# First stage of a two-layer hybrid decoder: weight and modulation loads issued a quarter at a time

## The chip, the cores and the metric

The kernel runs on 1 core of one Trainium2 chip. The metric is the device time of one execution in microseconds (us); lower is better.

## The reference

Two layers, each with a token mixer and a gated MLP. Every sub-layer is wrapped in RMSNorms and modulated by shift, scale and gate, which come from a conditioning vector. All inputs are float32. What matters here is the beginning of layer 0:

```python
cond = jax.nn.silu(c)
mods = cond @ w_ada[l] + b_ada[l]
sh1, sc1, g1, sh2, sc2, g2 = [m[:, None, :] for m in jnp.split(mods, 6, axis=-1)]
h = rms_norm(x, norm_pre_mix[l]) * (1.0 + sc1) + sh1
proj = h @ w_in
```

`x` is 256 x 2048, `w_ada[l]` is 2048 x 12288, `w_in` is 2048 x 4564. The columns of `proj` go to four head groups: latent attention, S5 (a diagonal complex state space model), sparse attention and gated DeltaNet. The S5 group also needs tables that depend on parameters alone.

## The kernel before

The order of instructions on each engine is made by a scheduler from the order in which the program writes them, their dependencies and priorities; `order` below means its result. Each engine and each DMA queue then works in that order. All large loads are issued on SP's queue, as tiles of 128 x 1024 floats (512 KB).

**Modulation.** No column of `h` can be made before shift and scale are known, so the first stage works in four quarters of the model dimension, 512 columns each. `ada_quarter(q)` (L490) loads the 16 tiles of `w_ada` for quarter `q` (8 MB) and multiplies each on TensorE with the condition vector into a bank (`mx`, products 32x512); after the last tile ScalarE copies the bank (`hf<-mx`, L513), four small products with `ident2` turn it into columns, and `ada_out` (L521) adds biases into `mod`. It is a generator: it issues a tile's load and writes the tile's products right behind it, and yields after every second tile. The tiles lie in free pieces of the arena and in the pools `rawa`, `rawm` and `acc`, two buffers each.

**Norm.** `row_scale` (L606) loads `x` transposed (`xT`, four tiles), squares it on ScalarE (two buffers), sums it with products with `ones` on TensorE, takes the inverse root on VectorE and scales the four quarters of `xT` (`scale`, L621). `norm_quarter(q)` (L628) applies shift and scale to a quarter (`hf`) and splits it in a high and a low part (`ht`), by a cast on ScalarE (L423) and a subtraction on VectorE (L424).

**First products.** `first_gemms(0)` (L1475) multiplies five column blocks of `w_in` (the list `FIRST`), each by one weight tile per quarter: `gemms_b` (L730) calls `wtile`, that is `wload` (L402, a load into one of four `raw` buffers) and `wsplit` (L437, a cast into one of three `wh` buffers and a subtraction into one of three `wl`), and then 24 products 128x256 into `mm` (the fifth block into `mx`). With `tiles=True` it yields after each weight tile.

**The loop.** `run` (L1675) puts these together. For quarters 1 to 3 it interleaves them by hand: after each of the five weight tiles it steps the modulation generator of the next quarter once or twice, and the generators of the S5 tables (`s5_tables`, L1241) and rotations (`s5_rotations`, L1364, all on VectorE at line L1367) twice. The five weight tiles of quarter 3 are left to `mixers` (L1481), which begins with what is left of the first products, and goes on with 852-column loads of `w_in` for other head groups. From there on the modulation tiles of the other blocks are summed on VectorE in the background (`ada`, L467).

Of the kernel before, what the change touches and what calls it, by code (L numbers as in the profile page):

```python
# [21 lines left out]
P = 128  # L22
# [38 lines left out]
FIRST = (O_U, O_U + 256, O_GQ, O_GK, O_GV)  # L61
# [21 lines left out]
class Blocks:  # L83
# [3 lines left out]
    def __init__(self):  # L87
        self.at, self.n = {}, 0
# [104 lines left out]
class Ker:  # L193
    def __init__(self, ctx, tc, I, out):
        self.tc, self.nc, self.I, self.out = tc, tc.nc, I, out
        pool = lambda name, bufs, **kw: ctx.enter_context(tc.tile_pool(name=name, bufs=bufs, **kw))
        self.const = pool("const", 1)
        self.ar = self.const.tile([P, NA], F32, name="arena")
        self.x = self.ar[:, A_X:A_X + 4096].rearrange("p (t d) -> p t d", t=2)

        ht = self.const.tile([P, 8, 1024], F32, name="ht")
        self.ht = [ht[:, i] for i in range(8)]
        self.raw = pool("raw", 4)
        self.whp = pool("wh", 3)
        self.wlp = pool("wl", 3)
        self.rawa = pool("rawa", 2)
        self.rawm = pool("rawm", 2)
        self.accp = pool("acc", 2)
        self.small = pool("small", 2)
        self.mmp = pool("mm", 4, space=PSUM)  # L210
        self.mxp = [pool("mx%d" % i, 2, space=PSUM) for i in range(2)]
        self.lane = None
        self.turn = 0
        self.turn_ins, self.turn_tiles = (), 0
        self.norm_ins, self.add_rest = (), None
        self.bg = iter(())
        self.side = iter(())
        self.boost = 0
        self.bg_rate = 0.0
        self.rates = (0.0,) * 4  # L220
        self.bg_credit = 0.0
# [268 lines left out]
    def ada_quarter(self, q):  # L490

        nc = self.nc
        bank = self.mx()
        pools = ((self.rawa, "rawa"), (self.rawm, "rawm"), (self.accp, "acc"))
        free = [A_OT + 1024] + (AT[7:9] if q else []) + (AT[:4] if q < 3 else [])
        for kc in range(KT):
            n = kc % (len(free) + 6)
            if n < len(free):  # L500
                w = self.reg(free[n], 1024)(1024)
            else:
                pool, nm = pools[(n - len(free)) % 3]
                w = pool.tile([P, 1024], F32, name=nm, tag=nm)
            nc.sync.dma_start(w, self.blk("w_ada", 0, kc, 1, (q * 512, 512), (D + q * 512, 512)))
            for i in range(2):
                o = 64 * (kc % 2) + 32 * i
                self.mm(bank[o:o + 32], self.condz[:, kc], w[:, i * 512:(i + 1) * 512], kc < 2, kc >= KT - 2)
            if kc % 2 and kc < KT - 1:
                yield  # L510
        with self.first():
            r = self.small.tile([P, 512], F32, name="hf", tag="hf")
            nc.scalar.copy(r, bank)  # L513
            cols = self.mx(8)
            for c in range(4):
                self.mm(cols[:, 2 * c:2 * c + 2], r[:, c * P:(c + 1) * P], self.ident2[:, 0:64:32], True, True)
            cols = cols.rearrange("p (c i) -> p i c", i=2)
            for i in range(2):
                self.ada_out(0, 2 * i + q // 2, cols[:, i], 4 * (q % 2))
# [210 lines left out]
    def gemms_b(self, l, cols, nm, kc, tiles=False):  # L730


        kn = 1024 // (nm * P)
        parts = [[b[:, m * 256:(m + 1) * 256] for m in range(nm)] for _, b in cols]
        for kk in range(0, KT, kc):
            for (c0, _), ps in zip(cols, parts):
                for k0 in range(kk, kk + kc, kn):
                    w = self.wtile(self.blk("w_in", l, k0, kn, (c0, nm * P)))
                    for ki in range(kn):
                        k = k0 + ki  # L740
                        for m in range(nm):
                            o = (ki * nm + m) * P
                            self.mm3(ps[m], [i[:, o:o + P] for i in w], self.hk(k), k == 0 and m == 0,
                                     k == KT - 1 and m == nm - 1)
                    if tiles:
                        yield
            if not tiles:
                yield
        return parts
# [725 lines left out]
    def first_gemms(self, l):  # L1475
        if l:
            return self.gemms_b(l, [(c, self.mmt()) for c in FIRST[:3]], 2, KT // 4)
        self.lane = 0
        return self.gemms_b(l, [(c, self.mmt() if i < 4 else self.mx()) for i, c in enumerate(FIRST)], 2, KT // 4, True)

    def mixers(self, l, first):  # L1481
# [193 lines left out]
    def run(self):  # L1675
# [13 lines left out]
        a = self.ada_quarter(0)  # L1689
        next(a)  # L1690
        self.finish(constants)
        self.lane = 0
        self.row_scale()
        self.lane = 1
        self.finish(a)
        done = self.norm_quarter(0)
        with self.after(done):
            for i in range(1, 4):
                self.scale(i)
        tables = self.s5_tables(0, nc.scalar, self.ar[:, AT[6]:AT[6] + 1024])  # L1700
        rotations = self.s5_rotations(0, (self.ar[:, AT[4]:AT[4] + 1024], self.ar[:, AT[5]:AT[5] + 1024]))
        g = self.first_gemms(0)
        for q in range(1, 4):
            self.lane = 1
            a = self.ada_quarter(q)
            if q == 3:
                self.lane = 0
                with self.after(done):
                    self.finish(tables)
                self.lane = 1  # L1710
            n = len(FIRST)
            for i in range(n):
                next(g)
                for _ in range(8 * (i + 1) // n - 8 * i // n):
                    next(a, None)
                self.lane = 0
                with self.after(done):
                    for _ in range(2):
                        next(tables if q < 3 else rotations, None)
                self.lane = 1  # L1720
            done = self.norm_quarter(q)
        self.lane = 0
        with self.after(done):
            self.finish(rotations)
# [5 lines left out]
        for l in range(DEPTH):  # L1730
            self.set_bg(bg[2 * l], False)
            if l:
                h, g = self.pre_norm(l, 0), self.first_gemms(l)
# [53 lines left out]
```

## Time and profile before

| | us |
|---|---|
| median of 3 runs | 2699.17 (2696.71 to 2700.51) |
| the profiled execution | 2692.16 |
| its span, first to last instruction | 2690.0 |
| TensorE busy | 2571.7 (96%) |
| VectorE busy | 1910.7 (71%) |
| ScalarE busy | 1259.9 (47%) |
| mean granted clock of TensorE | 0.978 |

The profile is of one execution. PE is TensorE, PEld its weight loads, DVE VectorE, ACT ScalarE, POOL GpSimd, SP the queue of loads (SPq). PEclk is the granted clock of TensorE in a stretch, 1.00 for 2.4 GHz and 0.50 for 1.2 GHz. A busy share of TensorE over the whole span says little about a stage: the first 200 us are looked at by stretches.

### The profile page before, as it was taken

The numbers are of one execution on the slowest core, as the hardware profiler recorded it, in microseconds if no ns is written. First come the engines' busy times: TensorE is split into PE (matmuls) and PEld (weight loads), VectorE is DVE, ScalarE is ACT, GpSimd is POOL, SyncE is SP. The second block draws the span as 40 slices with busy tenths as digits, with TensorE's granted clock in tenths as the row PEclk, the third lists the DMA queues.
The fourth block names the chain that finished last, engine by engine and source line by source line (L and its number), as shares of the span: only waits on it lengthen the run. The fifth ranks groups of instructions, "written<-read, shape, count | busy, mean of one in ns | idle before, by whom it ended". The sixth has DMA issues, their size and how long they took to land. (4 is left out here: it accounts for less than half of the span.)

```text
span 2690.0 us, 44478 instructions
## 1 busy us (share of the span) xinstructions
PE 2571.7 (96%) x17604; PEld 2285.0 (85%) x17604; DVE 1910.7 (71%) x3014; ACT 1259.9 (47%) x2002; POOL 10.1 (0%) x22
## 2 busy tenths in 40 slices
PE   7979998888999999999998999999899999999998
PEld 4568786767999999988887879888899999998886
DVE  5568867878787778776877888865776655555555
ACT  3344454555445444454545445465544444444443
POOL 0000000000000000000000000000000000000000
PEclk9989998889999999999998999999999999999999
DMA  8765756676888888876676567735587655555554
GB/s 343 313 212 198 256 197 210 220 266 216 291 297 277 289 289 298 291 242 234 229 269 216 176 218 248 254 114 180 186 283 270 209 185 183 182 184 186 185 189 147
DMA packets 171264, 620.89 MB, mean 231 GB/s; under 512 B 19440, under 2 KB 20272, under 8 KB 169520
## 3 DMA queue, kind: packets, MB, share of 16 engines
q1 hardware_dynamic: 170048, 617.00, 67.1%
q8 instruction: 138, 2.26, 0.3%
q10 hardware_dynamic: 1008, 1.06, 0.1%
q14 instruction: 70, 0.57, 0.1%
HBM read 613.75 MB, written 4.23 MB: 230 GB/s over the span
## 5 line engine op out<-in xcount | busy, mean ns | idle before, releaser
L228 PE MATMUL mm<-ht,wh 128*128 128x256 f32 x7168 | 1314.9, 284 | 6.7 <-ACT ht L423 5.8
L423 ACT CAST wh<-raw 128x1024 fp32r<-128x1024 f32 (+1 forms) x740 | 771.5, 1043 | 960.9 <-PE mm L228 785.0
L424 DVE TENSOR_TENSOR wl<-raw,wh 128x1024 fp32r<-128x1024 f32 (+1 forms) x740 | 896.6, 1214 | 404.5 <-ACT wh L423 401.0
L228 PEld LDWEIGHTS mm<-ht,wh 128*128 128x128 f32 x7168 | 1112.3, 189 | 22.8 <-issue 7.6
L228 PE MATMUL mm<-ht,wl 128*128 128x256 f32 x3584 | 1018.1, 284 | 2.4 <-DVE wl L424 2.4
L228 PEld LDWEIGHTS mm<-ht,wl 128*128 128x128 f32 x3584 | 675.3, 188 | 10.5 <-DVE wl L424 6.2
L228 PE MATMUL mm<-wh,ht 128*128 128x512 f32 (+1 forms) x1600 | 508.0, 396 | 8.0 <-ACT ht L423 4.2
L462 DVE SCALAR_TENSOR_TENSOR acc<-rawa,condc,acc 128x1024 f32<-128x1024 f32 x300 | 384.6, 1282 | 138.2 <-DMA rawa<-in_w_ada_dram 136.8
L228 PEld LDWEIGHTS mm<-wh,ht 128*128 128x128 f32 x1600 | 303.1, 191 | 72.3 <-ACT ht L423 4.5
L228 PE MATMUL mm<-wl,ht 128*128 128x512 f32 (+1 forms) x800 | 316.2, 395 | 0.0
L228 PE MATMUL mx<-arena 128*128 128x128 f32 (+9 forms) x1576 | 235.1, 320 | 18.9 <-DVE arena L373 10.0
L228 PEld LDWEIGHTS mx<-arena 128*128 128x128 f32 (+5 forms) x1576 | 164.8, 169 | 72.5 <-issue 20.4
L228 PE MATMUL mx<-wh,ht 128*128 128x512 f32 x704 | 222.3, 396 | 0.0
L228 PEld LDWEIGHTS mm<-wl,ht 128*128 128x128 f32 x800 | 152.6, 191 | 31.5 <-issue 0.2
L228 PEld LDWEIGHTS mx<-wh,ht 128*128 128x128 f32 x704 | 132.6, 188 | 32.3
L228 PE MATMUL mx<-wl,ht 128*128 128x512 f32 x352 | 139.5, 396 | 0.0
L424 DVE TENSOR_TENSOR ht<-arena,ht 128x1024 fp32r<-128x1024 f32 x52 | 63.6, 1223 | 40.4 <-ACT ht L423 40.1
L1615 DVE SCALAR_TENSOR_TENSOR arena<-mm,vec,arena 128x255 f32<-128x255 f32 (+1 forms) x176 | 78.5, 478 | 6.2 <-ACT arena L1613 5.3
L423 ACT CAST ht<-arena 128x1024 fp32r<-128x1024 f32 x52 | 54.2, 1049 | 56.1 <-PE mm L228 30.5
L228 PEld LDWEIGHTS mx<-wl,ht 128*128 128x128 f32 x352 | 66.3, 188 | 16.2
L232 PE MATMUL mx<-ident,arena 128*128 128x128 f32 (+1 forms) x328 | 59.4, 287 | 13.4 <-ACT arena L815 5.5
L232 PEld LDWEIGHTS mx<-ident,arena 128*128 128x128 f32 (+1 forms) x328 | 38.4, 144 | 29.9 <-ACT arena L815 9.8
(314 smaller groups left out, 1516.4 us busy)
## 6 DMA issues: line engine op xcount, KB each, us to landing
raw<-in_ffn_w_in_dram SPq DMA_DIRECT2D x352, 512.0 KB, 4.2
rawa<-in_w_ada_dram SPq DMA_DIRECT2D x330, 512.0 KB, 5.0
raw<-in_ffn_w_out_dram SPq DMA_DIRECT2D x176, 512.0 KB, 4.3
raw<-in_w_in_dram SPq DMA_DIRECT2D x116, 512.0 KB, 4.3
raw<-in_w_out_dram SPq DMA_DIRECT2D x64, 512.0 KB, 4.1
arena<-in_w_ada_dram SPq DMA_DIRECT2D x36, 512.0 KB, 7.8
raw<-in_w_in_dram SPq DMA_DIRECT2D x32, 426.0 KB, 3.9
rawm<-in_w_ada_dram SPq DMA_DIRECT2D x9, 512.0 KB, 9.3
```

Of the source, the lines that this page charges most:

```text
L228: self.nc.tensor.matmul(out, lhsT=lhsT, rhs=rhs, start=start, stop=stop)
L232: self.nc.tensor.transpose(out, in_, self.ident[:k, :k])
L423: self.nc.scalar.copy(hi.bitcast(F32R), src)
L424: self.last_lo = self.nc.vector.tensor_sub(lo.bitcast(F32R), src, hi)
L462: self.nc.vector.scalar_tensor_tensor(acc, w, self.condc[:, kc:kc + 1], acc, op0=ALU.mult, op1=ALU.add)
L1615: nc.vector.scalar_tensor_tensor(c[:, s:], ps[m][:, :256 - s], self.fconv(l, 2 - s, f), c[:, s:], op0=ALU.mult, op1=ALU.add)
```

## The change

`ada_quarter` issues all its 16 loads at once and yields, before any product; a tile takes a pool buffer by `kc % 3`, and only the pool buffers are used more than once. `run` now does the following for each quarter: norm the quarter, issue its five `w_in` loads (kept in `self.pre`, from which `gemms_b` takes them), issue the 16 modulation loads of the next quarter, and then interleave products as before. Quarter 3's loads of `w_in` are issued in the loop as well, and its products still in `mixers`. `first_gemms(0)` is made ahead of `row_scale`, so that its banks are taken first. The S5 tables are stepped in quarters 0 and 1 and finished there, the rotations in quarter 2; at the end of either of the last two quarters up to 16 steps are taken at once.

```diff
--- before.py
+++ after.py
@@ -216,6 +216,7 @@
         self.bg = iter(())
         self.side = iter(())
         self.boost = 0
+        self.pre = []
         self.bg_rate = 0.0
         self.rates = (0.0,) * 4
         self.bg_credit = 0.0
@@ -494,15 +495,18 @@
         nc = self.nc
         bank = self.mx()
         pools = ((self.rawa, "rawa"), (self.rawm, "rawm"), (self.accp, "acc"))
+        tiles = []
         free = [A_OT + 1024] + (AT[7:9] if q else []) + (AT[:4] if q < 3 else [])
         for kc in range(KT):
-            n = kc % (len(free) + 6)
-            if n < len(free):
-                w = self.reg(free[n], 1024)(1024)
+            if kc < len(free):
+                w = self.reg(free[kc], 1024)(1024)
             else:
-                pool, nm = pools[(n - len(free)) % 3]
+                pool, nm = pools[kc % 3]
                 w = pool.tile([P, 1024], F32, name=nm, tag=nm)
             nc.sync.dma_start(w, self.blk("w_ada", 0, kc, 1, (q * 512, 512), (D + q * 512, 512)))
+            tiles.append(w)
+        yield
+        for kc, w in enumerate(tiles):
             for i in range(2):
                 o = 64 * (kc % 2) + 32 * i
                 self.mm(bank[o:o + 32], self.condz[:, kc], w[:, i * 512:(i + 1) * 512], kc < 2, kc >= KT - 2)
@@ -735,7 +739,7 @@
         for kk in range(0, KT, kc):
             for (c0, _), ps in zip(cols, parts):
                 for k0 in range(kk, kk + kc, kn):
-                    w = self.wtile(self.blk("w_in", l, k0, kn, (c0, nm * P)))
+                    w = self.wsplit(self.pre.pop(0) if self.pre else self.wload(self.blk("w_in", l, k0, kn, (c0, nm * P))))
                     for ki in range(kn):
                         k = k0 + ki
                         for m in range(nm):
@@ -1475,7 +1479,6 @@
     def first_gemms(self, l):
         if l:
             return self.gemms_b(l, [(c, self.mmt()) for c in FIRST[:3]], 2, KT // 4)
-        self.lane = 0
         return self.gemms_b(l, [(c, self.mmt() if i < 4 else self.mx()) for i, c in enumerate(FIRST)], 2, KT // 4, True)
 
     def mixers(self, l, first):
@@ -1690,35 +1693,35 @@
         next(a)
         self.finish(constants)
         self.lane = 0
+        g = self.first_gemms(0)
         self.row_scale()
         self.lane = 1
         self.finish(a)
-        done = self.norm_quarter(0)
-        with self.after(done):
-            for i in range(1, 4):
-                self.scale(i)
         tables = self.s5_tables(0, nc.scalar, self.ar[:, AT[6]:AT[6] + 1024])
         rotations = self.s5_rotations(0, (self.ar[:, AT[4]:AT[4] + 1024], self.ar[:, AT[5]:AT[5] + 1024]))
-        g = self.first_gemms(0)
-        for q in range(1, 4):
-            self.lane = 1
-            a = self.ada_quarter(q)
+        n = len(FIRST)
+        for q in range(4):
+            done = self.norm_quarter(q)
+            if q == 0:
+                with self.after(done):
+                    for i in range(1, 4):
+                        self.scale(i)
+
+            self.pre = [self.wload(self.blk("w_in", 0, 4 * q, 4, (c0, 256))) for c0 in FIRST]
             if q == 3:
-                self.lane = 0
-                with self.after(done):
-                    self.finish(tables)
-                self.lane = 1
-            n = len(FIRST)
+                break
+            a = self.ada_quarter(q + 1)
+            next(a)
             for i in range(n):
                 next(g)
                 for _ in range(8 * (i + 1) // n - 8 * i // n):
                     next(a, None)
                 self.lane = 0
                 with self.after(done):
-                    for _ in range(2):
-                        next(tables if q < 3 else rotations, None)
+                    for _ in range(2 if q < 1 or i < n - 1 else 16):
+                        next(tables if q < 2 else rotations, None)
                 self.lane = 1
-            done = self.norm_quarter(q)
+            self.finish(a)
         self.lane = 0
         with self.after(done):
             self.finish(rotations)
```

SP's queue at the program's beginning, before (`xT` is the input that the row statistics need, `acc`, `rawa` and `rawm` are pools for modulation tiles):

```order
L505 DMA arena<-in_w_ada_dram 128x1024 x2
L611 DMA arena<-in_xT_dram 128x1024 x4
L505 DMA arena<-in_w_ada_dram 128x1024 x3
L505 DMA rawa<-in_w_ada_dram 128x1024
L505 DMA rawm<-in_w_ada_dram 128x1024
L505 DMA acc<-in_w_ada_dram 128x1024
```

and now, from the tenth of the 16 modulation tiles of quarter 0 on:

```order
L506 DMA rawm<-in_w_ada_dram 128x1024
L506 DMA acc<-in_w_ada_dram 128x1024
L506 DMA rawa<-in_w_ada_dram 128x1024
L615 DMA arena<-in_xT_dram 128x1024 x4
L506 DMA arena<-in_w_ada_dram 128x1024
L407 DMA raw<-in_w_in_dram 128x1024 x5
L506 DMA arena<-in_w_ada_dram 128x1024 x5
L506 DMA rawm<-in_w_ada_dram 128x1024
L506 DMA acc<-in_w_ada_dram 128x1024
```

The four `xT` loads stood behind two modulation tiles and now stand behind all 16 of the quarter. The five `w_in` loads of quarter 0 stand together; the next rows are modulation tiles of quarter 1.

SP's queue at the end of the stage, before (the four pool tiles are the last of quarter 3's modulation; the first of the six `raw` loads is quarter 2's, the other five are quarter 3's, and the 852-column ones belong to `mixers`):

```order
L505 DMA acc<-in_w_ada_dram 128x1024
L505 DMA arena<-in_w_ada_dram 128x1024 x3
L406 DMA raw<-in_w_in_dram 128x1024 x6
L406 DMA raw<-in_w_in_dram 128x852 x2
L505 DMA rawa<-in_w_ada_dram 128x1024
L505 DMA rawm<-in_w_ada_dram 128x1024
L505 DMA acc<-in_w_ada_dram 128x1024
L505 DMA rawa<-in_w_ada_dram 128x1024
```

and now:

```order
L506 DMA rawa<-in_w_ada_dram 128x1024
L506 DMA rawm<-in_w_ada_dram 128x1024
L506 DMA acc<-in_w_ada_dram 128x1024
L506 DMA rawa<-in_w_ada_dram 128x1024
L407 DMA raw<-in_w_in_dram 128x1024 x5
L1407 DMA arena<-in_s_w_glu_dram 128x2048
L407 DMA raw<-in_w_in_dram 128x852 x4
```

The last modulation tiles of quarter 3 stood behind seven loads that are used after them, and now stand ahead of all these.

VectorE at the row statistics and the first norm, before (lines L254 to L256 are the inverse root, L623 is the scaling of the first quarter, L638 the norm, `wl` the low part of a weight tile):

```order
L254 TENSOR_TENSOR arena_58<-arena_58 128x256
L255 TENSOR_TENSOR arena_58<-arena_58 128x256
L256 SCALAR_TENSOR_TENSOR arena_58<-arena_58 128x256
L623 TENSOR_TENSOR arena_58<-arena_58 128x1024
L526 TENSOR_TENSOR mod_90<-mx1_256,vec_115 128x4 x2
L530 SCALAR_TENSOR_TENSOR mod_90<-mod_90,vec_115 128x4
L638 TENSOR_SCALAR hf_264<-arena_58,mod_90 128x256 x2
L638 TENSOR_SCALAR hf_269<-arena_58,mod_90 128x256 x2
L424 TENSOR_TENSOR wl_285<-raw_282,wh_284 128x1024
```

and now (each line number is up by 1 to 4):

```order
L255 TENSOR_TENSOR arena_58<-arena_58 128x256
L425 TENSOR_TENSOR wl_324<-raw_287,wh_323 128x1024
L256 TENSOR_TENSOR arena_58<-arena_58 128x256
L425 TENSOR_TENSOR wl_393<-raw_289,wh_392 128x1024
L257 SCALAR_TENSOR_TENSOR arena_58<-arena_58 128x256
L425 TENSOR_TENSOR wl_446<-raw_291,wh_445 128x1024
L255 TENSOR_TENSOR arena_58<-arena_58 128x256
L256 TENSOR_TENSOR arena_58<-arena_58 128x256
L257 SCALAR_TENSOR_TENSOR arena_58<-arena_58 128x256
L255 TENSOR_TENSOR arena_58<-arena_58 128x256
```

One subtraction for a weight tile stood behind the first norm; now three stand inside the inverse root, ahead of it.

## Rows read from the trace of the kernel before

**Rows 1.** Busy time by stretch: us of each engine (x instructions), clock, DMA share, GB/s.
```profile
36.60:77.10 40.50, 37.68 (x241) 22.61 (x241) 28.05 (x89) 19.05 (x43) 0.00 (x0) 0.88 0.79 305
77.10:109.20 32.10, 28.26 (x227) 19.56 (x224) 8.88 (x20) 12.88 (x28) 0.00 (x0) 0.98 0.70 281
141.60:158.30 16.70, 6.73 (x27) 1.74 (x26) 3.07 (x9) 2.28 (x4) 0.00 (x0) 0.78 0.86 306
200.00:400.00 200.00, 199.33 (x1375) 168.41 (x1374) 161.05 (x299) 97.03 (x183) 0.52 (x1) 1.00 0.65 217
```

**Rows 2.** Timeline, TensorE: start us, us, operation, count, [idle before <-releaser].
```profile
36.59 0.58 PE L228 MATMUL mm<-ht,wh 128*128 128x256 f32 x1 [1.95 <-ACT ht L423]
...
66.17 3.42 PE L228 MATMUL mx<-arena 128*32 128x512 f32 x31
...
77.09 0.54 PE L228 MATMUL mm<-ht,wh 128*128 128x256 f32 x2
...
104.06 1.46 PE L228 MATMUL mx<-arena 128*32 128x512 f32 x9
...
109.24 0.58 PE L228 MATMUL mm<-ht,wh 128*128 128x256 f32 x1 [1.94 <-ACT ht L423]
...
148.81 1.92 PE L228 MATMUL mx<-rawa,arena 128*32 128x512 f32 x4 [6.82 <-DMA rawa<-in_w_ada_dram]
...
153.56 1.05 PE L228 MATMUL mx<-rawa,arena 128*32 128x512 f32 x4 [0.18 <-DMA rawa<-in_w_ada_dram]
...
158.29 0.63 PE L228 MATMUL mm<-ht,wh 128*128 128x256 f32 x3 [1.94 <-ACT ht L423]
```

**Rows 3.** Timeline, SP's queue: start us, us, load, count.
```profile
122.62 21.86 SPq L406 DMA_DIRECT2D raw<-in_w_in_dram  x8
144.57 0.38 SPq L505 DMA_DIRECT2D rawa<-in_w_ada_dram  x1
```

**Rows 4.** Timeline, TensorE, before the first weight tile's products.
```profile
11.87 9.55 PE L228 MATMUL mx<-arena,ones 128*128 128x256 f32 x32
...
25.47 1.05 PE L228 MATMUL mx<-acc,arena 128*32 128x512 f32 x4 [0.20 <-DMA acc<-in_w_ada_dram]
...
31.85 1.05 PE L228 MATMUL mx<-arena 128*32 128x512 f32 x4 [0.22 <-DMA arena<-in_w_ada_dram]
33.59 1.05 PE L228 MATMUL mx<-ident,hf 128*128 128x2 f32 x8 [0.69 <-ACT hf L513]
```

**Rows 5.** Timeline, VectorE, the row statistics and the first norm.
```profile
21.45 0.42 DVE L619 TENSOR_SCALAR arena<-mx 128x256 f32<-128x256 f32 x1 [6.53 <-PE mx L228]
...
26.84 1.23 DVE L623 TENSOR_TENSOR arena<-arena 128x1024 f32<-128x1024 f32 x1
...
35.15 1.38 DVE L638 TENSOR_SCALAR hf<-arena,mod 128x256 f32<-128x256 f32 x4
```

**Rows 6.** Line L424 to 158 us: count, ns min/median/max, first and last start.
```profile
L424 DVE TENSOR_TENSOR wl<-raw,wh x18: 1218/1222/1226, 36.4 to 142.9; 128x1024 fp32r<-128x1024 f32 x18
```

**Rows 7.** Timeline, TensorE: weight tile products at both clocks; modulation tiles grouped and alone.
```profile
39.55 0.63 PE L228 MATMUL mm<-ht,wh 128*128 128x256 f32 x2
...
40.19 0.63 PE L228 MATMUL mm<-ht,wh 128*128 128x256 f32 x2
...
45.14 0.40 PE L228 MATMUL mm<-ht,wh 128*128 128x256 f32 x2
...
45.50 0.40 PE L228 MATMUL mm<-ht,wh 128*128 128x256 f32 x2
...
47.75 1.92 PE L228 MATMUL mx<-arena 128*32 128x512 f32 x16
...
55.34 1.05 PE L228 MATMUL mx<-rawm,arena 128*32 128x512 f32 x4
```

**Rows 8.** DMA issues of the whole run: count, KB each, median us to landing.
```profile
raw<-in_w_in_dram SPq DMA_DIRECT2D x116, 512.0 KB, 4.3
```

**Rows 9.** VectorE by line, 105 to 140 us: busy us, mean ns | idle before.
```profile
L1367 DVE TENSOR_TENSOR arena<-arena 128x16 f32<-128x16 f32 (+6 forms) x42 | 18.3, 462 | 0.8
```

**Rows 10.** Busy time by stretch, layer 0's mixers and what follows.
```profile
400.00:700.00 300.00, 260.61 (x1667) 225.73 (x1666) 238.24 (x494) 156.40 (x324) 3.23 (x3) 0.91 0.69 234
```

## The prediction

> **What bounds the kernel now.** I read the stretches first. From 200 us on TensorE is busy 199.33 of 200 us [rows 1]: time won before that point is kept only if this later work simply begins earlier. In the first stage it is not so: between 141.6 and 158.3 us TensorE is busy 6.73 of 16.7 us.
>
> The timeline of TensorE says why. The stage has four quarters, and the products of the five weight tiles of a quarter begin at 36.59, 77.09, 109.24 and 158.29 us [rows 2]. The quarters last 40.5, 32.1 and 49.1 us. The last is the odd one: at 148.81 TensorE has waited 6.82 us for a modulation tile in `rawa`, and the last of them is multiplied at 153.56. SP's queue shows where that tile was: eight `w_in` loads take from 122.62 until 144.48, and only at 144.57 is the `rawa` load issued [rows 3]. Those eight loads need `raw` buffers. The buffers come free when tiles are cast, the casts need `wh` buffers, and these wait for products of the last quarter, which wait for the modulation tiles behind the eight loads. So a queue in the wrong order bounds the last quarter, not the transfers' rate: with the queue full, one tile of 512 KB follows another every (31.85 - 25.47) / 5 = 1.28 us [rows 4].
>
> **The change, part by part.** The sum is made against the profiled execution, 2692.16 us, of which the stage up to the last quarter's products is 158.3. The median of the runs shown, 2699.17, is 7.0 us above it; I subtract the gain from the median.
>
> **The last quarter's tiles.** The order now has all modulation tiles of quarter 3 ahead of that quarter's five `w_in` loads and ahead of the 852-column loads. Nothing that waits for quarter 3's products stands ahead of its inputs. That removes the cause of the 16.7 us hole, of which 3.7 us stay: from the last modulation product (153.56 + 1.05) to 158.29 the bank is copied, spread, normed and cast, and quarter 2 shows the same, 104.06 + 1.46 to 109.24.
>
> **The start.** `xT` moves behind all 16 modulation tiles, so the row statistics come later. Before, the sixteenth tile was the twentieth transfer and TensorE took it at 31.85; now it is the sixteenth: 31.85 - 4 x 1.28 = 26.7, its products until 27.8, copy and four small products 1.7 us more (33.59 + 1.05 - 32.90) [rows 4], 29.5. Then come the products with `ones`, which took 9.55 us [rows 4]: 39.0. Bounds: they cannot end before the last `xT` tile, four transfers after the last modulation tile (31.8), with a square and its products behind it (1.3 us), 33.1; and at half clock they could take a few us more. I take 39.0, since ScalarE and TensorE alternate on the same two buffers as before. VectorE's root takes 26.84 - 21.45 = 5.4 us [rows 5], and now three `wl` subtractions stand inside it, 1.22 us each [rows 6]: 3.7. Then the scaling 1.2, and 36.59 - 35.15 = 1.4 us from the norm to the first product. Sum: 50.7, that is 14.1 us later than before. This delay is TensorE's, and I find no cover for it; only two modulation tiles of quarter 1 are multiplied in it.
>
> **Quarter 0 to 1.** Three products of a weight tile take 0.36 us at full clock (45.14 to 45.50) and 0.64 at the half level (39.55 to 40.19) [rows 7]. Five tiles of eight such steps are 14.4 us. I keep a slow beginning of 6 us as before (2.7 us lost), since TensorE idles ahead of it again. A modulation tile costs 0.48 us in a dense group (1.92 / 4) and 1.05 alone [rows 7]: 14 tiles in some five groups, 14 x 0.48 + 5 x 0.57 = 9.6. From the last of them (66.17 + 3.42) to 77.09 lay 7.5 us, with the S5 tables on ScalarE and VectorE inside, and they stand there in the new order too. Together 34.2, with half a us for table products 34.7; before it was 40.5, in which TensorE was busy 37.68 [rows 1]. Quarter 1 begins at 85.4.
>
> **Quarter 1 to 2.** The same products and the same table work as before, with a grouping slightly denser: 31.5 for 32.1 us. It begins at 116.9.
>
> **Quarter 2 to 3.** 14.4 us of weight tiles; eight modulation tiles alone among them, 8 x 1.05 = 8.4; seven more behind, 7 x 0.48 = 3.4; 3.7 to the first product of quarter 3. That is 29.9. The 13 tiles of this quarter that use pool buffers have six of them, so the last ones are loaded only when earlier ones were multiplied, and a load on a queue that is not full takes 4.3 us to land [rows 8]. The last such round ends some 2 us after TensorE could take it: 32. Quarter 3 begins at 148.9, against 158.29: **9.4 us won**.
>
> **A wait that is added.** The fifth `w_in` load of each quarter needs the buffer of the first, and so that tile's cast and subtraction, which VectorE does behind the quarter's norm. Behind that load SP holds 15 modulation tiles. So per quarter the transfers need 1.2 + 4.3 + 15 x 1.28 = 24.7 us after the quarter's first product; TensorE needs 26.2 for its own part. It is hidden, by 1.5 us only. The Trainium skill (DMA: Bandwidth & Descriptors, Bandwidth, where 436 GB/s comes from) holds that HBM to SBUF transfers are bound by the HBM side, about 358 GB/s; the rows' 524,288 bytes in 1.28 us are 410, so this trace does not agree. By the rule a tile would take 1.46 us, the 24.7 would be 27.4, an estimate, and the sum would lose about 1.2 us.
>
> **VectorE.** The rotation tables, 42 operations of 18.3 us [rows 9], now all stand ahead of quarter 3's norm. VectorE has them and five subtractions (6.1 us) to do in the 28 us before that norm: hidden, with 3 us to spare. Background sums move out of the hole into work where TensorE is busy; I cost them at nothing, as there are slots on VectorE from 200 to 400.
>
> **The rivals.**
>
> *More is won.* If the `ones` products end at the lower bound, 33.1, and quarters 1 and 2 take 30 us, quarter 3 begins at about 139: 18 to 20 us won, 2680. For it: the transfers alone would allow far less than I sum. Against: TensorE's own work per quarter.
>
> *Nothing is left.* If the start costs half as much again (7 us more: `xT` late, `ones` at the half clock level), quarter 3 begins at 156 and 2 us remain: about 2697. For it: TensorE is nearly idle ahead of them. Against: they took 9.55 us directly after a cold start as well.
>
> *Slower.* The scheduler makes a new order for layer 0's mixers too, not only for the stage. Between 400 and 700 us TensorE is idle 39.4 of 300 us [rows 10], in waits for VectorE and ScalarE among filler products. If the new order places the fillers worse and this idle time grows by half, 20 us, it outweighs the 9.4 and the run ends 10 us later: 2710. It decides from 15 us on. For it: the orders differ up to there. Against: the same waits stand in the same places of the program.
>
> *The change does not do what it says.* The order shows that it does on SP.
>
> **How the numbers follow.** A measurement of this kernel can tell about 0.2%, 5.4 us, from no change. The forecast (6 to 14 us won) has 0.52, more won 0.17, nothing left 0.21 (this holds 2694 to 2704), slower 0.10. The predicted time is that of the forecast: 2699.2 - 9.4 = 2690. Its own range is 2685 to 2693. The range of 8 in 10 takes in most of the cases beside it, 2677 to 2701. Faster 0.69, same 0.21, slower 0.10.
>
> **What would show it.** In the changed profile: the first products of the quarters near 51, 85, 117 and 149 us; no wait of TensorE for `rawa` above 2 us before quarter 3; on SP no stretch over 10 us in which 852-column loads hold modulation tiles; short halts at the fifth `w_in` load of each quarter; and TensorE's busy time from 400 to 700 us near 261. Wrong would be: a first product near 40 us (the start costs nothing), or quarter 3 at 156 or later, or a lead at 200 us that is gone at 700.

## The result, and the profile after

The change makes the kernel slower: 2714.90 us median of 4 runs (2708.78 to 2716.56), against 2698.02 for the kernel before, run beside it. The ratio is 1.0058, 95% interval 1.0040 to 1.0076. The forecast was 9 us won; 16 to 17 us are lost. The profiled execution has a span of 2714.8 us at a mean granted clock of 0.973.

TensorE's timeline of the changed kernel has the products with `ones` and the first products of the four quarters (idle time ahead of a row and what ended it in brackets), to be read against [rows 2]:

```profile
28.45 7.70 PE L229 MATMUL mx<-arena,ones 128*128 128x256 f32 x32
...
47.27 1.31 PE L229 MATMUL mm<-ht,wh 128*128 128x256 f32 x4 [1.45 <-ACT ht L424]
...
82.20 0.79 PE L229 MATMUL mm<-ht,wh 128*128 128x256 f32 x2 [1.62 <-ACT wh L424]
...
117.54 0.80 PE L229 MATMUL mm<-ht,wh 128*128 128x256 f32 x2 [2.55 <-ACT wh L424]
...
148.64 1.05 PE L229 MATMUL mx<-acc,arena 128*32 128x512 f32 x4 [1.16 <-DMA acc<-in_w_ada_dram]
149.88 1.05 PE L229 MATMUL mx<-rawa,arena 128*32 128x512 f32 x4 [0.19 <-DMA rawa<-in_w_ada_dram]
...
154.61 0.58 PE L229 MATMUL mm<-ht,wh 128*128 128x256 f32 x1 [1.94 <-ACT ht L424]
```

Quarter 3 begins at 154.61 instead of 158.29: 3.7 us won, not 9.4. In the ten runs below that leave the stage as it is, quarter 3 begins between 152.0 and 156.0 us, so one profile gives this start to some 2 us. SP's queue shows that the old fault is gone and what came in its place:

```profile
23.23 16.06 SPq L407 DMA_DIRECT2D raw<-in_w_in_dram  x5
39.40 2.55 SPq L506 DMA_DIRECT2D arena<-in_w_ada_dram  x5
...
68.59 2.27 SPq L506 DMA_DIRECT2D arena<-in_w_ada_dram  x3
83.43 0.33 SPq L407 DMA_DIRECT2D raw<-in_w_in_dram  x1
...
132.42 0.33 SPq L506 DMA_DIRECT2D rawa<-in_w_ada_dram  x1
135.15 0.33 SPq L506 DMA_DIRECT2D rawm<-in_w_ada_dram  x1
...
144.40 0.33 SPq L506 DMA_DIRECT2D acc<-in_w_ada_dram  x1
145.81 0.33 SPq L506 DMA_DIRECT2D rawa<-in_w_ada_dram  x1
146.23 9.81 SPq L407 DMA_DIRECT2D raw<-in_w_in_dram  x5
```

No `w_in` load of quarter 3 stands ahead of a modulation tile now (146.23 is behind 145.81). But the five loads of a quarter stop the queue at the fifth (23.23 to 39.29, and from 70.86 to 83.43), and the last modulation tiles of quarter 3 leave one at a time, 1.4 to 2.7 us apart, seven from 132.42 to 145.81.

So the stage is shorter, and the loss lies behind it. Here are the stretches of the changed kernel (columns as in [rows 1]):

```profile
200.00:400.00 200.00, 196.15 (x1353) 165.57 (x1352) 154.85 (x278) 94.05 (x179) 0.53 (x1) 0.99 0.63 212
400.00:600.00 200.00, 163.82 (x976) 135.83 (x975) 150.19 (x369) 99.36 (x231) 3.23 (x3) 0.86 0.61 205
600.00:700.00 100.00, 81.95 (x518) 73.78 (x517) 81.05 (x128) 51.11 (x88) 0.00 (x0) 0.88 0.70 244
```
And of the kernel before:

```profile
400.00:600.00 200.00, 169.80 (x1033) 141.09 (x1032) 156.85 (x364) 100.87 (x232) 3.23 (x3) 0.90 0.68 231
600.00:700.00 100.00, 90.81 (x636) 84.64 (x635) 81.39 (x130) 55.53 (x93) 0.00 (x0) 0.95 0.70 241
700.00:1300.00 600.00, 596.60 (x4553) 567.62 (x4552) 464.65 (x520) 280.01 (x369) 0.00 (x0) 1.00 0.80 276
```

TensorE's idle time from 400 to 700 us is 54.2 us (36.2 and 18.0); before it was 39.4 [rows 10]. The first load of layer 0's output weights was issued at 381.59 us, 9.0 us ahead of before (390.56); the first load of the gated MLP at 621.26, 5.8 us behind (615.46); the first of its second weights at 1172.10, 19.0 behind (1153.09); the spans end 24.8 us apart. (These are single executions: the profiled one before is 5.9 us below the median of 2698.02 and the one after 1.7 us above its own; the medians are 16.9 us apart. The stretches are cut by time and not by work, so they don't hold quite the same products.)

The clearest place is the end of layer 0's mixer. `residual` reduces the sums of squares, takes two inverse roots on VectorE in small steps, and makes `diag`, for which TensorE waits. VectorE's timeline of the changed kernel there:

```profile
639.56 0.18 DVE L687 TENSOR_REDUCE bt<-bs 128x6 f32<-128x24 f32 x1
640.10 1.28 DVE L463 SCALAR_TENSOR_TENSOR acc<-rawa,condc,acc 128x1024 f32<-128x1024 f32 x1 [0.36 <-DMA rawa<-in_w_ada_dram]
...
643.15 1.28 DVE L463 SCALAR_TENSOR_TENSOR acc<-rawa,condc,acc 128x1024 f32<-128x1024 f32 x1
...
644.93 1.28 DVE L463 SCALAR_TENSOR_TENSOR acc<-rawa,condc,acc 128x1024 f32<-128x1024 f32 x1
...
647.98 1.28 DVE L463 SCALAR_TENSOR_TENSOR acc<-rawa,condc,acc 128x1024 f32<-128x1024 f32 x1
...
649.24 0.47 DVE L577 TENSOR_SCALAR diag<-ident,cy 128x128 f32<-128x128 f32 x2
...
652.28 1.23 DVE L482 STREAM_TRANSPOSE acc<-acc 128x1024 f32<-128x1024 f32 x1
...
660.77 1.21 DVE L484 TENSOR_REDUCE acc<-acc 128x32 f32<-128x1024 f32 x1
```

Between the reduction (L687) and `diag` (L577) stand four background sums of modulation (L463), 4 x 1.28 = 5.1 us, so that 9.7 us pass. Before, the last sum began at 620.11, and the same chain took 4.8 us, in VectorE's timeline of the kernel before:

```profile
620.11 1.29 DVE L462 SCALAR_TENSOR_TENSOR acc<-rawa,condc,acc 128x1024 f32<-128x1024 f32 x1 [1.29 <-DMA rawa<-in_w_ada_dram]
...
633.25 0.18 DVE L683 TENSOR_REDUCE bt<-bs 128x6 f32<-128x24 f32 x1 [0.97 <-ACT junk L660]
...
638.07 0.47 DVE L573 TENSOR_SCALAR diag<-ident,cy 128x128 f32<-128x128 f32 x2
```

TensorE's timeline of the changed kernel has the wait for `diag`. The profile names no releaser for it (`issue`); that it is `diag` is read from the operands and the times, 649.24 for `diag` and 650.48 for the first product that reads it:

```profile
650.48 3.97 PE L229 MATMUL mx<-diag,arena 128*128 128x128 f32 x16 [14.72 <-issue]
...
662.03 0.23 PE L229 MATMUL mx<-acc,ident 128*32 128x8 f32 x2 [2.99 <-DVE acc L484]
```
And of the kernel before:

```profile
639.30 3.11 PE L228 MATMUL mx<-diag,arena 128*128 128x128 f32 x13 [9.19 <-issue]
```

The background block also ends inside this stretch (transpose at 652.28, reduction at 660.77), and TensorE waits for it as well at 662.03.

**Theory and rivals.** `wload` steps the background generator each time it issues a load (`self.tick(self.bg_rate)`). The five `w_in` loads of quarter 3 were issued in `mixers`, where the rate is 0.5: 2.5 steps. The change issues them in the loop of the first stage, where the rate is still 0: no step. Counted in the program, eight sums of layer 0's blocks were left for the end of the mixer, and now eleven; the half step stays in `bg_credit`, so that all later steps fall half a step elsewhere. Theory 1: these lost steps cost the time. Rival A: the loss comes from the new stage or the loads that run ahead. What bounds the stage, the late `xT` or SP's halts, is a question of its own (B, S and Q below).

### The profile page after: what moved, and what is told of

Same layout as the page of the kernel before. It is cut to its first block, busy times and chain, and to the rows that moved or that the text cites. A ratio compares the mean times of both kernels' runs of the same rounds, so it can differ in the third digit from the quotient of the medians.

```text
span 2714.8 us, 44475 instructions
## 1 busy us (share of the span) xinstructions
PE 2576.9 (95%) x17604; PEld 2291.2 (84%) x17604; DVE 1912.8 (70%) x3014; ACT 1261.1 (46%) x2004; POOL 10.2 (0%) x22
## 5 line engine op out<-in xcount | busy, mean ns | idle before, releaser
L424 ACT CAST wh<-raw 128x1024 fp32r<-128x1024 f32 (+1 forms) x740 | 771.5, 1044 | 971.7 <-PE mm L229 819.5
L463 DVE SCALAR_TENSOR_TENSOR acc<-rawa,condc,acc 128x1024 f32<-128x1024 f32 x300 | 384.4, 1281 | 141.9 <-DMA rawa<-in_w_ada_dram 140.6
L229 PE MATMUL mx<-arena 128*128 128x128 f32 (+8 forms) x1520 | 220.3, 308 | 24.6 <-DVE gea L1072 9.3
L229 PEld LDWEIGHTS mx<-arena 128*128 128x128 f32 (+5 forms) x1520 | 159.3, 168 | 69.5 <-issue 18.2
L1618 DVE SCALAR_TENSOR_TENSOR arena<-mm,vec,arena 128x254 f32<-128x254 f32 (+1 forms) x176 | 78.0, 476 | 5.5 <-ACT arena L1616 4.4
L424 ACT CAST ht<-arena 128x1024 fp32r<-128x1024 f32 x52 | 54.2, 1049 | 57.2 <-PE mm L229 31.7
L233 PE MATMUL mx<-ident,arena 128*128 128x128 f32 (+1 forms) x328 | 60.6, 295 | 20.2 <-ACT arena L1111 4.8
```

The costliest lines, as they stand in the source:

```text
L229: self.nc.tensor.matmul(out, lhsT=lhsT, rhs=rhs, start=start, stop=stop)
L233: self.nc.tensor.transpose(out, in_, self.ident[:k, :k])
L424: self.nc.scalar.copy(hi.bitcast(F32R), src)
L463: self.nc.vector.scalar_tensor_tensor(acc, w, self.condc[:, kc:kc + 1], acc, op0=ALU.mult, op1=ALU.add)
L1618: nc.vector.scalar_tensor_tensor(c[:, s:], ps[m][:, :256 - s], self.fconv(l, 2 - s, f), c[:, s:], op0=ALU.mult, op1=ALU.add)
```

## Experiments

Ratios are to the kernel before, run beside each, with 95% intervals. "us" is the median.

### Steps put back, and steps taken away

The steps alone, put back in the changed kernel (`gemms_b`):

```diff
+                    if self.pre:
+                        self.tick(self.bg_rate)
                     w = self.wsplit(self.pre.pop(0) if self.pre else self.wload(...))
```

> The changed kernel with one thing put back: when a weight tile is taken from the list of tiles loaded ahead, the background generator is stepped by the current rate, as a load issued at that point did before (no effect in the stage, where the rate is 0; 2.5 steps in the mixers of layer 0). Theory 1 (lost background steps): the stage is as in the changed kernel (quarter 3 near 154.6 us), the last background block of layer 0 ends ahead of the residual chain, no background sum stands between the residual's reduction and the two diag operations, TensorE's wait for diag is near 9 us instead of 14.7, the first load of the gated MLP is issued near 606 us (621.3 in the changed kernel), and the time falls by 10 to 20 us, to 2695 to 2705. Rival A (the loss comes from the stage itself or from loads that now run ahead in the mixers, not from the steps): the time stays within 5 us of the changed kernel's 2714.9.

2691.54 us, 0.9983 (0.9974 to 0.9992): 23 us below the changed kernel, where 10 to 20 were expected, and a little below the kernel before. The stretches of that run:

```profile
400.00:600.00 200.00, 168.79 (x985) 138.85 (x984) 155.09 (x358) 98.45 (x230) 3.23 (x3) 0.87 0.66 227
600.00:700.00 100.00, 91.84 (x660) 86.59 (x659) 82.22 (x130) 56.55 (x93) 0.00 (x0) 0.95 0.68 240
```
And its wait for `diag` in TensorE's timeline:

```profile
633.50 6.50 PE L229 MATMUL mx<-diag,arena 128*128 128x128 f32 x32 [8.16 <-issue]
```

The wait is 8.16 us instead of 14.72, and from 600 to 700 us TensorE is idle 8.2 us, not 18.0; from 400 to 600 it is 31.2, not 36.2. The stage is the changed one, with quarter 3 at 152.62. The steps are the cause; rival A falls.

The mirror, in the kernel before: the five loads don't step.

```diff
+                    rate, self.bg_rate = self.bg_rate, 0.0 if tiles else self.bg_rate
                     w = self.wtile(self.blk("w_in", l, k0, kn, (c0, nm * P)))
+                    self.bg_rate = rate
```

> The kernel before with one thing taken away: the five weight tiles of quarter 3, loaded in the mixers, do not step the background generator (2.5 steps fewer). Stage as before (quarter 3 at 158 us). Theory 1 (lost background steps alone cost the time): 10 to 20 us slower than before, 2708 to 2718. Rival A: within 4 us of before. Between the two: the late steps cost only where the scheduler then places the left-over sums in the residual chain, and here the time is 2 to 8 us above before.

2715.91 us, 1.0075 (1.0054 to 1.0097): the whole loss, without any change of the stage. But its order has no sum between the reduction and `diag`; here the time goes elsewhere, as its stretches show:

```profile
400.00:600.00 200.00, 158.68 (x968) 131.76 (x967) 149.65 (x368) 95.01 (x225) 3.23 (x3) 0.87 0.62 214
700.00:1300.00 600.00, 588.68 (x4548) 562.51 (x4547) 451.12 (x506) 268.08 (x346) 0.00 (x0) 0.99 0.77 272
```

41.3 us idle from 400 to 600 (30.2 before), in the waits of the mixers' serial chains (10.2 us for `arena` of L817 on ScalarE, for which the kernel before waited 5.3 at L815, is the largest that grew), and 11.3 from 700 to 1300 (3.4 before). So sums in the residual chain are one form of the price, not its cause.

### The start and SP's queue

`xT` behind the second modulation tile again, without and with the steps:

```diff
             tiles.append(w)
+            if q == 0 and kc == 1:
+                xT = self.ar[:, A_X:A_X + 4096]
+                for i in range(4):
+                    nc.sync.dma_start(xT[:, i * 1024:(i + 1) * 1024], self.I["xT"][:, i * 1024:(i + 1) * 1024])
```

(and the same loads taken out of `row_scale`)

> The changed kernel with the four xT loads issued behind the second modulation tile again instead of behind the sixteenth. If the late xT is what makes the start late, the first product of quarter 0 comes at 37 to 41 us instead of 47.3. Theory 1: the gain reaches quarter 3 (146 to 149 instead of 154.6) and then the end, 2704 to 2710, with the residual chain of layer 0 still disturbed. Rival B (the quarters are bound by SP's queue, which halts at the fifth weight load, not by the start): quarter 3 stays within 3 us of 154.6 and the time within 4 us of 2714.9.

> Both edits together in the changed kernel: background steps put back and xT early. Theory 1: the two gains add, quarter 3 near 147, first load of the gated MLP near 600 us, time 2685 to 2697, below the kernel before. Rival A: no better than xT early alone, 2704 or more.

2725.20 us, 1.0111 (1.0094 to 1.0129), and 2702.53, 1.0024 (1.0014 to 1.0035): an early `xT` makes it 10 to 11 us slower, in either. The steps are worth 22.7 us here too, with another order of the stage. Quarter 0 begins at 40.58 in the second, but quarter 1 only at 89.83 and quarter 3 at 164.53. SP's queue of that run (the one with the steps):

```profile
15.43 0.33 SPq L506 DMA_DIRECT2D rawm<-in_w_ada_dram  x1
24.07 0.33 SPq L506 DMA_DIRECT2D acc<-in_w_ada_dram  x1
```
TensorE of the same run:

```profile
16.40 4.95 PE L229 MATMUL mx<-arena,ones 128*128 128x256 f32 x20
...
40.58 0.80 PE L229 MATMUL mm<-ht,wh 128*128 128x256 f32 x2 [1.76 <-ACT wh L424]
...
56.38 1.05 PE L229 MATMUL mx<-arena 128*32 128x512 f32 x4
...
58.27 1.05 PE L229 MATMUL mx<-arena 128*32 128x512 f32 x4
```

The products with `ones` now stand ahead of modulation products on TensorE (16.40), so the pool buffers come free late and SP halts from 15.76 to 24.07; and in the new order the tiles of quarter 1 stand singly among the weight products, 1.05 us each, where the late `xT` has groups of four tiles in 1.92 us, as in TensorE's timeline of the changed kernel:

```profile
57.76 1.92 PE L229 MATMUL mx<-arena 128*32 128x512 f32 x16
```

Both theories were wrong: the start is earlier and the end later. Again with the steps, `xT` behind the fourteenth tile (the diff with `kc == 13`):

> The changed kernel with the background steps put back and the xT loads issued behind the fourteenth modulation tile of quarter 0 instead of behind the sixteenth. The two last modulation tiles wait for pool buffers, xT does not. If the order of TensorE stays dense (the groups of modulation products are nearly those of the run with the background steps alone), quarter 0 begins at 44 to 47 us and the time is within 4 us of 2691.5, unlike xT behind the second tile (2702.5). Rival: every earlier xT costs, 2696 or more.

2691.78 us, 0.9988 (0.9977 to 0.9999): nothing changes, with quarter 3 at 153.65.

The fifth load of a quarter moved behind the thirteenth modulation tile, with the steps:

```diff
-            self.pre = [self.wload(self.blk("w_in", 0, 4 * q, 4, (c0, 256))) for c0 in FIRST]
+            self.pre = [self.wload(self.blk("w_in", 0, 4 * q, 4, (c0, 256))) for c0 in (FIRST if q == 3 else FIRST[:4])]
...
             tiles.append(w)
+            if q and kc == 12:
+                self.pre.append(self.wload(self.blk("w_in", 0, 4 * q - 4, 4, (FIRST[4], 256))))
```

> The changed kernel with the background steps put back, and the fifth weight load of quarters 0 to 2 issued behind the thirteenth modulation tile of the next quarter, not ahead of the first. Theory S (the fifth load, which waits for a buffer, holds the modulation tiles behind it on SP, and that is why quarters 0 to 2 are longer than forecast): TensorE's wait of 6.6 us for a modulation tile at 37 us goes, quarter 1 begins 3 to 7 us earlier than 81.7 us, quarter 3 at 146 to 150 us instead of 152.6, time 2684 to 2689. Rival Q (the quarters are as long as TensorE's order and the pool buffers make them): quarter 3 within 2 us of 152.6 and the time within 3 us of 2691.5.

2688.81 us, 0.9965 (0.9952 to 0.9978), not to be told from the run with the steps alone. TensorE's wait for a tile at 37 us falls from 6.6 to 2.6 us, and quarter 2 begins at 112.46 instead of 115.74. But quarter 3 does not move (152.62 with the steps alone), in TensorE's timeline:

```profile
152.75 1.66 PE L229 MATMUL mm<-ht,wh 128*128 128x256 f32 x4 [2.96 <-ACT ht L424]
```

Quarters 0 and 1 together are some 3 us shorter, and quarter 2 is as much longer. The moved load now stands behind a modulation tile that waits for a pool buffer. SP's queue of that run has quarter 2's:

```profile
134.78 0.42 SPq L407 DMA_DIRECT2D raw<-in_w_in_dram  x1
```
And in TensorE's timeline of the run TensorE waits for its cast:

```profile
141.24 0.51 PE L229 MATMUL mx<-ht,wh 128*128 128x256 f32 x2 [2.44 <-ACT wh L424]
```

Rival Q holds for the end of the stage.

### Number of steps, their phase, and what follows

The two halves of the lost steps apart: only the credit corrected behind layer 0's mixers of the changed kernel, and only the credit spoilt in the kernel with the steps.

```diff
             self.drain()
+            if l == 0:
+                self.bg_credit -= 0.5
```

> The changed kernel with the background credit set back by 0.5 after layer 0's mixers: eleven sums are left over at their end, as in the changed kernel, but from the gated MLP of layer 0 on the background steps fall where they fell before. Theory 1a (two separate prices: sums in layer 0's residual chain, and steps shifted by half a step in all that follows): the first load of the gated MLP stays near 621 us, but nothing more is lost behind it, so the end comes about 19 us earlier, 2694 to 2703. Theory 1b (the price is paid in layer 0's mixers and what follows from them): 2710 to 2718, and the lag grows after 621 us as in the changed kernel.

(and `+= 0.5` with the steps)

> The mirror of the run with the credit set back: background steps put back in the mixers, but the credit is raised by 0.5 after them, so that all later steps fall where they fall in the changed kernel. Theory 1a: first load of the gated MLP near 610.6 us, then 13 to 19 us are lost up to the end, 2704 to 2711. Theory 1b: within 4 us of 2691.5.

2707.46 us, 1.0042 (1.0030 to 1.0054), and 2698.28, 1.0007 (0.9996 to 1.0019). By the medians the half step behind the mixers is worth about 7 us in both directions (2714.9 - 2707.5, and 2698.3 - 2691.5); only the second is clear of the intervals, the first is not (1.0030 to 1.0054 overlaps 1.0040 to 1.0076). The other 16 us go with the steps that are missing in layer 0's mixers. Neither theory was right alone: the end came 7 us earlier and not 19, and with the credit set back the lag to the kernel with the steps grew, in the two profiled executions, from 8.4 us at the first load of the gated MLP to 25.5 at the first of its second weights.

Then the number of steps put back, as a factor:

```diff
-                        self.tick(self.bg_rate)
+                        self.tick(0.2 * self.bg_rate)
```

The factors are 0.2, 0.6, 1.4, 1.8 and 3; -0.2 takes half a step away (eleven left over, with the old fraction of the credit), and 0.4 with the credit corrected as above gives ten with the other fraction.

> As the run with the background steps put back, but only 0.2 of each step: 0.5 steps instead of 2.5, so ten sums are left over at the end of layer 0's mixers, not eight, with the credit as before. The order has no sum between the residual's reduction and diag. Theory C (what costs is sums inside the residual chain): 2688 to 2698, TensorE's wait for diag near 9 us. Theory N (what costs is that fewer steps are done early, three to two sums too few): 2702 to 2710.

> 0.6 of each step put back: 1.5 steps, nine sums left over. Here the order has three sums and the transpose inside the residual chain. Theory C: slower than the run with ten left over, 2700 to 2710, wait for diag 12 us or more. Theory N: between the runs with ten and with eight left over, 2694 to 2703.

> 1.8 of each step: 4.5 steps, six sums left over; no sum in the residual chain. Theory C: as with eight left over, 2688 to 2696. Theory N: faster still than 2691.5, 2680 to 2688.

> 3 of each step: 7.5 steps, three sums left over; no sum in the residual chain. Theory C: 2688 to 2698. Theory N: 2675 to 2686.

> Eleven sums left over, as in the changed kernel, but the credit's fraction in the mixers of layer 0 is that of the kernel before (half a step is taken away, none put back); the credit after the mixers is as before. Theory P (the phase: at which loads the steps fall): 2690 to 2700. Theory N11 (the number left over): as the run with only the credit set back, 2703 to 2711.

> Ten sums left over, and the fraction in the mixers is that of the changed kernel; the credit is set back after the mixers. Theory P: 2702 to 2710. Theory N11: as the other run with ten left over, 2692 to 2700.

> 3.5 steps put back, seven sums left over. If the time falls smoothly towards six: 2685 to 2691. If each count makes an order of its own: anywhere between 2684 and 2702, most likely 2690 to 2698.

| sums left over | us | ratio, 95% interval | TensorE idle 400-600, 600-700 us |
|---|---|---|---|
| 11 (credit corrected) | 2707.46 | 1.0042, 1.0030 to 1.0054 | 36.7, 20.2 |
| 11, old fraction | 2703.98 | 1.0029, 1.0016 to 1.0043 | 34.6, 17.9 |
| 10 | 2696.70 | 1.0001, 0.9990 to 1.0013 | 34.9, 9.9 |
| 10, other fraction | 2695.66 | 0.9997, 0.9987 to 1.0008 | 24.6, 22.4 |
| 9 | 2693.97 | 0.9988, 0.9974 to 1.0002 | 27.1, 19.2 |
| 8 (all steps) | 2691.54 | 0.9983, 0.9974 to 0.9992 | 31.2, 8.2 |
| 7 | 2690.64 | 0.9982, 0.9971 to 0.9992 | 29.9, 10.6 |
| 6 | 2684.63 | 0.9952, 0.9933 to 0.9971 | 25.4, 8.3 |
| 3 | 2700.50 | 1.0007, 0.9993 to 1.0022 | 33.7, 10.9 |

Behind the mixers all of these step alike. From eleven to six the medians fall with every sum done earlier, from 2704.0 to 2684.6, by 1 to 7 us each. The whole of it is clear of noise, and so is the step from eleven to ten; from seven to six the intervals touch, and the steps between lie within them. The fraction moves the median by 3.5 us at most, within the intervals, so theory P falls. The kernel with nine left over settles the residual chain: it has sums there, and TensorE waits 16.26 us ahead of the products of the background block, which stands in the chain, and then 1.39, by its timeline:

```profile
638.90 0.42 PE L229 MATMUL mx<-acc,ident 128*32 128x8 f32 x16 [16.26 <-DVE cy L273]
640.71 4.46 PE L229 MATMUL mx<-diag,arena 128*128 128x128 f32 x23 [1.39 <-issue]
```

yet it is fast: from 400 to 600 it lost 9 us less than the changed kernel. The run with ten left over and the other fraction says the same: TensorE waits 15.64 us for `diag`, and it takes 2695.66. Theory C falls, and so does theory N in its simple form: with three left over TensorE is idle 33.7 us from 400 to 600 again, and the time rises.

Last, the two edits that were best alone, six left over and the fifth load later:

> 4.5 steps put back (six left over) and the fifth weight load behind the thirteenth modulation tile. If the gains add: 2680 to 2684. If the stage's small gain is lost behind quarter 3: 2683 to 2689.

2698.38 us, 1.0006 (0.9995 to 1.0017): they don't add, and neither range holds. The medians are 13.8 us apart, with the same number left over; from 400 to 600 us TensorE is busy 8.1 us less. The stretch with the six alone:

```profile
400.00:600.00 200.00, 174.63 (x1026) 144.54 (x1025) 157.28 (x375) 100.68 (x231) 3.23 (x3) 0.87 0.66 228
```
And with the load moved too:

```profile
400.00:600.00 200.00, 166.54 (x994) 138.23 (x993) 148.52 (x357) 100.63 (x232) 3.23 (x3) 0.87 0.62 211
```

## Why the prediction was wrong

**The step that failed** is one clause: "Background sums move out of the hole into work where TensorE is busy; I cost them at nothing". I took the sums to be moved. In fact five calls lost what they did beside loading: they no longer stepped the generator. I counted the DMAs of the moved loads and not their `tick`. Putting it back takes 23 us off, taking it away elsewhere adds 20.

**The rival "Slower"** had the place and nearly the price: it said that idle time of TensorE from 400 to 700 us grows by half of 39.4 and the run ends at 2710. It grew by 14.8 us, and the run ended at 2715. What set it off here was three sums more left over; with the steps put back the same stage gives back 260.63 busy us of 300 in that stretch, as before [rows 10]. That a new order can cost as much by itself, as the rival had it, the runs show too: the early `xT` (10 to 11 us) and the fifth load with six left over (13.8 us) don't change the number. The sign that would show the prediction wrong, a lead at 200 us that is gone at 700, is what the loads showed. A chance of 0.10 was too low for a mechanism whose program text I had in hand and did not follow to the tick.

**The start**: forecast 50.7, measured 47.27. The `ones` products took 7.70 us, not 9.55, and ended at 36.15, between the two bounds; the root with its three subtractions took 8.4 us (36.19 to 44.57), not 9.1. Right within 3.4 us.

**Quarter 0 to 1**: forecast 34.7, measured 34.9, in part by luck: up to the end of the last modulation product it took 25.6 us (26.7 forecast), and from there 9.3 (7.5).

**Quarter 1 to 2**: forecast 31.5, measured 35.3. The term is "The same products and the same table work as before". They are, but they took longer: TensorE is busy 30.9 us for 28.3 before [rows 1]. The quarter began at the lower clock level, where before it began at the higher. TensorE had been busy 7.6 of the 12.2 us ahead of it (70.00 to 82.20), and before 10.2 of 12.1 (65.00 to 77.09). The first 10 us of the quarter before, by stretches:

```profile
77.09:87.00 9.91, 8.69 (x89) 7.80 (x87) 3.42 (x9) 7.57 (x22) 0.00 (x0) 0.99 1.03 417
```
And in the changed kernel:

```profile
82.20:92.00 9.80, 9.43 (x66) 7.15 (x67) 4.54 (x6) 5.92 (x14) 0.00 (x0) 0.62 0.67 242
```

The fifth load held the queue to 83.43, 1.2 us behind the quarter's first product, as forecast (SP had stood there from 70.86), and it was hidden, as forecast: TensorE waits for no modulation tile from 82.20 to 117.54. With the load moved the quarter takes 33.2 (79.30 to 112.46) at a mean clock of 0.95 instead of 0.89.

**Quarter 2 to 3**: forecast 32, measured 37.1. The term is "14.4 us of weight tiles", a sum at full clock with no slow beginning, which the sum for quarter 0 has. The stretch of the changed kernel from the first product to the first single modulation tile:

```profile
117.54:126.82 9.28, 8.74 (x50) 8.31 (x50) 7.23 (x22) 3.02 (x4) 0.00 (x0) 0.67 0.73 277
```

50 products at full clock, three in 0.36 us [rows 7], would be 6.0 us, an estimate; they took 9.3, and 3.3 of the 5.1 us are here. The round of pool buffers came out as forecast: a tile leaves SP when TensorE has multiplied an earlier one (product of a `rawa` tile until 132.38, next `rawa` load at 132.42), and TensorE waits only 1.16 and 0.19 us for the last two, not 2. So of 9.4 us 3.7 remained, and with the steps put back the whole kernel is 4 us below the kernel before.

**Transfers**: from 26 to 40 us of the run with steps and early `xT` the core moved 390 GB/s. By the rule that the prediction priced, from the Trainium skill (DMA: Bandwidth & Descriptors, Bandwidth), the HBM side would have bound it at about 358 GB/s. The same section of the Trainium skill gives that figure for each core when both cores of the HBM domain stream, and up to 425 as measured on a single core. This kernel runs on one core, and the trace agrees with the second; the prediction took the rule without its condition.

## What to carry over

When a call is moved, follow what else it does: a load that also advances a counter or a generator takes that with it, and no view of the moved stage shows it. Count such steps in the program before and after (here 8 and 11 left over) before pricing the rest. Rates that were set for one order are worth another look after any move: six left over is the fastest version measured, 2684.63 us, 0.9952 of the kernel before, but as the last run shows, the best rate for one order is not the best for its neighbour. And where one quarter's sum has a slow beginning at the lower clock level, ask whether the others have one too: here two of them lost some 3 us each by it.

## What was not expected of the hardware

A hole costs more than its length. Here are 30 us around the residual chain, cut so that the first product with `diag` (650.48, and 633.50 with the steps) stands 10.5 us behind the start, in the changed kernel:

```profile
640.00:670.00 30.00, 16.20 (x99) 15.55 (x100) 26.30 (x64) 7.53 (x14) 0.00 (x0) 0.62 0.53 174
```
And in the one with the steps:

```profile
623.02:653.02 30.00, 21.84 (x169) 21.10 (x168) 25.76 (x70) 16.96 (x32) 0.00 (x0) 0.83 0.37 129
```

TensorE is idle 13.8 us and not 8.2, and does 99 products and not 169. 5.6 us of idle time more alone don't make that difference: the granted clock is 0.62, nearer to the 1.2 GHz level (0.50) than to the 2.4 GHz one, and 0.83 with the shorter hole, and the mean time of a product is 164 ns and not 129 (the mix of products differs somewhat). Over the span TensorE's busy time grew by 5.2 us (2576.9 for 2571.7 before) for the same 17604 products.

What stays open: by which chain each sum left over costs its time from 400 to 600 us was not followed one by one, and where the 7 us of the half step behind the mixers lie was not found; they were only measured.
